# Attention scores' low product over all 128 partitions, and the second selection of two token tiles tied to u tiles

## Chip, cores and metric

The kernel runs on one core of a Trainium2 chip. The metric is the device time of one execution in microseconds (us), as the median of several runs. The engines are named as in the profile: PE is TensorE's matmuls, PEld its weight loads, DVE is VectorE, ACT is ScalarE, POOL is GpSimd, SP issues DMAs. Each engine executes its own instructions in order and waits on semaphores of the others.

## What is computed

One layer of an encoder over 512 tokens (and 16 meta tokens) of width 1024: differential attention with 4 heads of twice 64 channels, a bidirectional gated linear attention beside it, an output projection, and then a feed-forward part that picks 16 of 16384 single-neuron experts for each token and head through product keys. Cut to what the change touches:

```python
s = jnp.einsum('bqhcd,bkhcd->bhcqk', qi, k).astype(jnp.float32)       # scores of the two halves c, d = 64
p = jax.nn.softmax(s, axis=-1)
a = p[:, :, 0] - lam * p[:, :, 1]
...
def peer_ffn(x, w_q, sub_keys, u, v):
    q = (xi @ w_q).reshape(n, PEER_HEADS, 2, PEER_KEY_DIM)
    s = jnp.einsum('nhpc,hpkc->nhpk', q, sub_keys).astype(jnp.float32)
    ts, ti = lax.top_k(s, PEER_TOPK)                                  # first selection: 16 of 128, twice
    cand_s = (ts[:, :, 0, :, None] + ts[:, :, 1, None, :]).reshape(n, PEER_HEADS, PEER_TOPK * PEER_TOPK)
    best_s, best_p = lax.top_k(cand_s, PEER_TOPK)                     # second selection: 16 of the sums
    idx = jnp.take_along_axis(cand_i, best_p, axis=-1)
    gate = jax.nn.softmax(best_s, axis=-1)
    act = jax.nn.gelu(jnp.einsum('nd,nhkd->nhk', xi, u[idx]).astype(jnp.float32), approximate=False)
    return jnp.einsum('nhk,nhkd->nd', (gate * act).astype(xi.dtype), v[idx])
```

## The kernel before

Precise products are made of three fast ones: a value is split into a rounded high part and the rest, the low part (ACT copies, then DVE or POOL subtracts: L118 and L120 for streamed weights), and high by high, high by low and low by high are added up in PSUM (`mm3`, L131 to L133).

The program has these stages. The front (to about 355 us) normalises, projects, and runs the attention (`attn_unit`, one for each of 4 heads and 4 tiles of 128 tokens) and the linear attention between the streamed projections, then the output projection. From there to about 470 us come the query projection of the feed-forward part and the first selection (`top16`: MAX8, FIND_INDEX8, MATCH_REPLACE8, MAX8, FIND_INDEX8 for each row). The u phase (470 to 765 us) multiplies three of the four token tiles with all experts: 60 u tiles of 24 matmuls in its first part (`u_tile`), whose streamed weights are split by DVE or, for the first `LP` of them, by POOL (`u_split`). The v phase (795 to 1606 us) multiplies the activations with the other expert matrix. Token tile 0 goes another way: its experts are gathered row by row by POOL's indirect DMAs, and DVE works on the rows.

For token tiles 1 to 3 the gates of the selected experts are spread into a dense matrix by matmuls with one-hot tiles. That is done by 48 building steps (`wbuild`) woven into the u tiles: step n of 8 tokens stands behind u tile `tgt(n)` = `A0` + int(0.56 n), and `AG` later from step n = `AL` = 14 on. A step needs one comparison and one product on DVE (`oh`, L1024 and L1029, four buffers), 16 matmuls on PE (L1060, L1063) and copies on ACT. The first step of a token tile transposes that tile's selection on PE (L1002: gate, row and column, from `sel`). Steps are prepared one ahead, so the transposes of tile 2 are asked for at the step with n = 15.

The second selection (`topk2`, L194) runs on DVE for two token tiles a and one half of the heads b at a time: a conversion (`tf`), three additions that make 80 candidates for each head, `top16` for each of 8 heads, some ten small row operations, then twice a comparison with 16 positions (L239), a product (L243), three halving additions (L245) and a write to `sel` (L247). Last the gate is made (`fin`, L250: an exponential on ACT, a sum, a reciprocal and a product, L255). Tiles 0 and 1 are one such pair (a = 0), of which the second half, (0, 1), is done ahead of the building steps; tiles 2 and 3 (`late`, L964 and L1043) are the pairs (1, 0) and (1, 1), written in the program between steps 13 and 14.

What sets the order: Tile's scheduler orders each engine's instructions by a simulated timeline and by the dependencies of data. Added dependencies of kind ORDER_DEP (`anchors[i]` is the last matmul of u tile i, `gelus[i]` its activation) only fix an order in that list.

In `attn_unit` each half c of a head has two matmuls into one bank: the low part of the keys over the 64 rows of that half (L490), then the high part over 128 rows (L491), where the query tile `stq` holds the high part in 64 rows and the low part in the other 64.

## Time and profile before

| | us |
|---|---|
| median of 3 runs (lowest, highest) | 1622.23 (1618.59, 1625.28) |
| the profiled execution | 1627.63 |
| its span | 1625.9 |
| PE busy | 1559.1 (96%) |
| DVE busy | 1265.5 (78%) |
| ACT busy | 714.2 (44%) |
| POOL busy | 538.0 (33%) |

The mean granted clock of TensorE is 0.981 of full speed. A share of busy time is a mean over stages with different limits, so the rows below are read by stretch. In a timeline the columns are start, duration, engine, line, operation, output and inputs, shapes; matmuls overlap in the pipeline, so what one costs is read from start to start. In square brackets stands how long the engine was idle ahead of a row, and what it waited for.

### The profile page before, as it was taken

Reading aid. Unit: us, or ns where it says so; the run is one execution under the profiler, and the core shown is the slowest. Engines: PE = TensorE matmul, PEld = TensorE weight load, DVE = VectorE, ACT = ScalarE, POOL = GpSimd, SP = SyncE. Lnnn points to the kernel's source line nnn. Section 1 sums busy time; section 2 is a strip of 40 time slices with the busy share of each in tenths; the row PEclk is TensorE's granted clock in tenths of the full one; section 3 lists DMA queues with packets and bytes.
Section 4 is the critical chain, followed back from the end, with each engine's and each line's share of the span. In section 5 each row is a group of like instructions: output and inputs, shape, how many; then the busy total and the mean of one; then the engine's idle time right before and its main releaser. Section 6 shows DMA issues by size and latency. Waiting matters only on the chain.

```text
span 1625.9 us, 24038 instructions
## 1 busy us (share of the span) xinstructions
PE 1559.1 (96%) x8793; PEld 1382.0 (85%) x8793; DVE 1265.5 (78%) x2492; ACT 714.2 (44%) x1131; POOL 538.0 (33%) x419
## 2 busy tenths in 40 slices
PE   6999999999996799998999999999999999999997
PEld 6887886778896799998888888889999999999996
DVE  3888767657999986993477777798878888788896
ACT  5444654544332476884333333333333333333333
POOL 3445113048553001000012222255445554344442
PEclk9999998999998899999999999999999999999998
DMA  6112122233233376879999988899999999999975
GB/s 234 61 48 84 59 61 70 81 108 106 92 128 112 115 264 228 309 285 341 338 312 304 328 321 286 290 388 343 351 346 333 331 339 346 351 324 339 335 256 181
DMA packets 152358, 387.40 MB, mean 238 GB/s; under 512 B 12752, under 2 KB 71376, under 8 KB 150576
## 3 DMA queue, kind: packets, MB, share of 16 engines
q1 hardware_dynamic: 104432, 213.62, 38.3%
q0 software_dynamic: 36864, 134.23, 22.9%
q10 hardware_dynamic: 10944, 38.02, 6.2%
q8 instruction: 69, 1.13, 0.3%
q14 instruction: 49, 0.40, 0.1%
HBM read 342.56 MB, written 40.63 MB: 236 GB/s over the span
## 4 chain that ended last, share of the span: by engine, by line
PE 73%; DVE 14%; DMA 5%; issue 3%; POOL 2%; ACT 2%; SPq 1%; POOLq 0%; ACTq 0%; DVEq 0%
PE bankg L131 10%; PE bankg L132 10%; PE bankg L133 10%; PE banka L1123 7%; PE banka L1122 7%; PE banka L1119 7%; PE bankp L1119 3%; PE bankp L1123 3%; PE bankp L1122 3%; PE banka L1060 1%; PE banka L1063 1%; POOL lo L120 1%; PE banka L656 1%; PE banka L491 1%; PE banka L490 1%
## 5 line engine op out<-in xcount | busy, mean ns | idle before, releaser
L264 POOL DMA_INDIRECT gat<-u,idx x128 | 166.3, 1300 | 568.8 <-PE bankp L1123 243.1
L118 ACT CAST hi<-raw 128x1024 fp32r<-128x1024 f32 x177 | 186.1, 1053 | 308.9 <-PE bankg L132 224.2
L131 PE MATMUL bankg<-un_hi,hi 128*128 128x384 f32 x896 | 302.9, 338 | 5.4 <-ACT act L1094 5.4
L133 PE MATMUL bankg<-un_hi,lo 128*128 128x384 f32 x896 | 302.3, 338 | 0.0
L132 PE MATMUL bankg<-un_lo,hi 128*128 128x384 f32 x896 | 302.0, 337 | 0.0
L120 DVE TENSOR_TENSOR lo<-raw,hi 128x1024 fp32r<-128x1024 f32 x142 | 174.0, 1227 | 97.8 <-ACT hi L118 96.1
L264 POOL DMA_INDIRECT gat<-v,idx x128 | 169.2, 1322 | 182.2 <-PE bankp L1123 155.0
L139 DVE TENSOR_TENSOR vhl<-vraw,vhl 128x1024 fp32r<-128x1024 f32 x128 | 156.3, 1221 | 51.6 <-ACT vhl L138 51.5
L278 DVE CUSTOM_DVE_ANT_0 gat<-gat,hn 128x1024 f32<-128x1024 f32 x128 | 155.2, 1221 | 42.3 <-DMA gat<-u,idx 42.2
L131 PEld LDWEIGHTS bankg<-un_hi,hi 128*128 128x128 f32 x896 | 169.4, 189 | 9.4 <-ACT act L1094 5.7
L138 ACT CAST vhl<-vraw 128x1024 fp32r<-128x1024 f32 x128 | 134.2, 1049 | 93.1 <-PE bankp L1123 53.2
L132 PEld LDWEIGHTS bankg<-un_lo,hi 128*128 128x128 f32 x896 | 169.3, 189 | 3.2
L133 PEld LDWEIGHTS bankg<-un_hi,lo 128*128 128x128 f32 x896 | 169.3, 189 | 1.7
L276 DVE SCALAR_TENSOR_TENSOR acc<-gat,sact,acc 128x1024 f32<-128x1024 f32 x128 | 163.9, 1280 | 5.0 <-DMA gat<-v,idx 4.0
L120 POOL TENSOR_TENSOR lo<-raw,hi 128x1024 fp32r<-128x1024 f32 x35 | 85.4, 2442 | 68.7 <-ACT hi L118 68.6
L1065 ACT ACTIVATE stg<-banka 128x512 f32<-128x512 f32 x96 | 96.3, 1171 | 11.7 <-PE banka L1063 10.5
L1094 ACT ACTIVATE act<-bankg 128x384 f32<-128x384 f32 x112 | 54.5, 486 | 32.3 <-PE bankg L133 27.2
L1024 DVE TENSOR_TENSOR oh<-iT,ioh 128x2048 f16<-128x2048 f16 x48 | 56.9, 1216 | 0.4 <-PE banka L1063 0.4
L1029 DVE TENSOR_TENSOR oh<-oh,gs 128x2048 f16<-128x2048 f16 x48 | 56.9, 1216 | 0.0
L1060 PE MATMUL banka<-oh 128*128 128x128 f16 x384 | 48.6, 220 | 0.9 <-ACT stg L1065 0.5
L131 PE MATMUL bankg<-act_hi,hi 128*128 128x264 f32 (+1 forms) x144 | 47.3, 328 | 1.3 <-ACT vN L777 1.3
L1063 PE MATMUL banka<-oh 128*128 128x128 f16 x384 | 48.2, 219 | 0.0
(2287 smaller groups left out, 3771.7 us busy)
## 6 DMA issues: line engine op xcount, KB each, us to landing
raw<-uT SPq DMA_DIRECT2D x128, 512.0 KB
vraw<-v SPq DMA_DIRECT2D x128, 512.0 KB
W_d<-stg ACTq DMA_DIRECT2D x12, 2048.0 KB
wa<-W_d SPq DMA_DIRECT2D x32, 768.0 KB
A_d<-act ACTq DMA_DIRECT2D x60, 192.0 KB
wa<-A_d SPq DMA_DIRECT2D x15, 768.0 KB
raw<-wq SPq DMA_DIRECT2D x16, 512.0 KB
raw<-win_n SPq DMA_DIRECT2D x12, 512.0 KB
```

Of the source, the lines that this page charges most:

```text
L118: nc.scalar.copy(hi, raw)
L120: (eng or nc.vector).tensor_sub(lo, raw, hi.bitcast(F32))
L131: nc.tensor.matmul(o, lhsT=ah, rhs=bh, start=start, stop=False)
L132: nc.tensor.matmul(o, lhsT=ah, rhs=bl, start=False, stop=False)
L133: return nc.tensor.matmul(o, lhsT=al, rhs=bh, start=False, stop=stop)
L139: (eng or nc.vector).tensor_sub(lo, src, hi.bitcast(F32))
L264: g = nc.gpsimd.indirect_dma_start(out=r, out_offset=None, in_=src, in_offset=bass.IndirectOffsetOnAxis(ap=idx[:, hk:hk + 1], axis=0))
L276: nc.vector.scalar_tensor_tensor(acc0, r, sact[:, hk:hk + 1], acc0, op0=ALU.mult, op1=ALU.add)
L278: nc.vector.tensor_tensor_reduce(r, r, hn0, scale=1.0, scalar=0.0, op0=ALU.mult, op1=ALU.add, accum_out=sact[:, hk:hk + 1])
L1119: m0 = nc.tensor.matmul(o, lhsT=gh_[:, tc_], rhs=vh[:, dc], start=(j == 0), stop=False, skip_group_check=True)
L1122: nc.tensor.matmul(o, lhsT=gh_[:, tc_], rhs=vl[:, dc], start=False, stop=False, skip_group_check=True)
L1123: m = nc.tensor.matmul(o, lhsT=gl_[:, tc_], rhs=vh[:, dc], start=False, stop=(j == NK - 1), skip_group_check=True)
```

## The change

1. The low part of the keys is written to `klz`, four tiles of 128 rows (one for each half, for two heads in turn), in which the other half's 64 rows are zeroed once at the beginning by POOL copies of zeros. The low product takes all 128 rows of the query tile. To make room, the pool tag `q` has 3 buffers instead of 4, `glan` lies inside `acc0`, and some small tiles (`mx`, `nb`, `zt`, `rz`, `sf`, `em`, `kmn`, not shown in the diff) have one buffer less.
2. The late second selections are tied: the conversion and the three additions of (1, 0) are ordered behind u tile 17 and those of (1, 1) behind u tile 22.
3. POOL subtracts for u tiles 0 to 11 and 18 to 28, instead of 0 to 13.
4. `A0` is 10 instead of 11 and `AG` 11 instead of 10: the building steps of tile 1 begin one u tile earlier, those behind `AL` stay.

```diff
@@ -51,7 +51,7 @@
 RB = 2
-TBUF = {'e': 3, 'g': 6, 'q': 4, 'x': 2}
+TBUF = {'e': 3, 'g': 6, 'q': 3, 'x': 2}
 GA = 4
@@ -77,10 +77,11 @@
 PG = 33, 49, 1
-LP = 14
-A0 = 11
+LP = 12
+LQ = 18, 29
+A0 = 10
 AR = 0.56
-AG = 10
+AG = 11
 AL = 14
@@ -191,15 +192,18 @@
-    def topk2(a, b, sm, cand, tf, eq, zs):
+    def topk2(a, b, sm, cand, tf, eq, zs, behind=None):
         ts_ = tsv[:, b, 2 * a:2 * a + 2].rearrange("p t h c r -> p (t h) c r")
         ti_ = tiv[:, b, 2 * a:2 * a + 2].rearrange("p t h c r -> p (t h) c r")
-        nc.vector.tensor_copy(tf, ti_[:, :, :, :, None].to_broadcast([P, PH, 2, TOPK, 2]))
-        nc.vector.tensor_add(cand[:, :, 0:16], ts_[:, :, 1, :], ts_[:, :, 0, 0:1].to_broadcast([P, PH, 16]))
-        nc.vector.tensor_add(cand[:, :, 16:72].rearrange("p h (a b) -> p h a b", b=8),
-                             ts_[:, :, 1, None, 0:8].to_broadcast([P, PH, 7, 8]),
-                             ts_[:, :, 0, 1:8, None].to_broadcast([P, PH, 7, 8]))
-        nc.vector.tensor_add(cand[:, :, 72:80], ts_[:, :, 0, 8:16], ts_[:, :, 1, 0:1].to_broadcast([P, PH, 8]))
+        ops = [nc.vector.tensor_copy(tf, ti_[:, :, :, :, None].to_broadcast([P, PH, 2, TOPK, 2])),
+               nc.vector.tensor_add(cand[:, :, 0:16], ts_[:, :, 1, :], ts_[:, :, 0, 0:1].to_broadcast([P, PH, 16])),
+               nc.vector.tensor_add(cand[:, :, 16:72].rearrange("p h (a b) -> p h a b", b=8),
+                                    ts_[:, :, 1, None, 0:8].to_broadcast([P, PH, 7, 8]),
+                                    ts_[:, :, 0, 1:8, None].to_broadcast([P, PH, 7, 8])),
+               nc.vector.tensor_add(cand[:, :, 72:80], ts_[:, :, 0, 8:16], ts_[:, :, 1, 0:1].to_broadcast([P, PH, 8]))]
+        if behind is not None:
+            for o_ in ops:
+                tc.add_manual_dep(o_.ins, anchors[behind], ORDER_DEP, reason="order")
         bsv = sm("bsv")
@@ -392,6 +396,11 @@
+    klz = [[f1.tile([P, T], F32R, name=f"klz{j}{c}") for c in range(2)] for j in range(2)]
+    for kz in klz:
+        for c in range(2):
+            nc.gpsimd.tensor_copy(kz[c][64 - 64 * c:128 - 64 * c], rrs[0][64 - 64 * c:128 - 64 * c, :T])
+
     def proj_rope(c, meta):
@@ -406,12 +415,12 @@
         st_ = [f2.tile([P, T], F32R, name=f"st{'qk'[meta]}{j}") for j in range(2)]
-        lo = f2.tile([P, T], F32R, name="stl") if meta else tz("sql", [P, T], F32R)
+        lo = klz[c % 2] if meta else [tz("sql", [P, T], F32R)] * 2
         for j in range(2):
...
             nc.scalar.copy(st_[j][r], dst[r, :T])
-            nc.gpsimd.tensor_sub(lo[r], dst[r, :T], st_[j][r].bitcast(F32))
-            nc.sync.dma_start(out=st_[j][x].bitcast(F32), in_=(st_[j] if meta else lo)[r].bitcast(F32))
+            nc.gpsimd.tensor_sub(lo[j][r], dst[r, :T], st_[j][r].bitcast(F32))
+            nc.sync.dma_start(out=st_[j][x].bitcast(F32), in_=(st_[j] if meta else lo[j])[r].bitcast(F32))
         return dst, st_, lo
@@ -448,7 +457,7 @@
     nc.vector.tensor_scalar(subw, subw, 1.0 - LAM0, None, op0=ALU.mult)
-    glan = f1.tile([P, P], F32, name="glan")
+    glan = acc0[:, D - P:]
     nc.sync.dma_start(out=glan, in_=I["glan"].to_broadcast([P, P]))
@@ -486,13 +495,12 @@
         for c in range(2):
-            rows = slice(64 * c, 64 * c + 64)
-            nc.tensor.matmul(s[c], lhsT=qs_[c][rows, qc], rhs=kl[rows, :], start=True, stop=False)
+            nc.tensor.matmul(s[c], lhsT=qs_[c][:, qc], rhs=kl[c], start=True, stop=False)
             nc.tensor.matmul(s[c], lhsT=qs_[c][:, qc], rhs=ks[c], start=False, stop=True)
@@ -925,12 +933,12 @@
-    def topk2w(a, b):
+    def topk2w(a, b, behind=None):
         def sm(name, dt=F32):
...
         return topk2(a, b, sm, tk2.tile([P, PH, NCAND], F32, name="cand"), tk2.tile([P, PH, 2, TOPK, 2], BF, name="tf"),
-                     tk1.tile([P, PH * 8, 2 * TOPK], BF, name="eq", tag="gat", bufs=GA), tk2.tile([P, PH], F32, name="zs"))
+                     tk1.tile([P, PH * 8, 2 * TOPK], BF, name="eq", tag="gat", bufs=GA), tk2.tile([P, PH], F32, name="zs"), behind)
@@ -1040,8 +1048,9 @@
             if n == AL:
-                for ab in late:
-                    for _ in topk2w(*ab):
+                for j, ab in enumerate(late):
+                    yield tgt(n) - AG + j * AG // 2
+                    for _ in topk2w(*ab, behind=tgt(n) - AG + j * AG // 2):
                         pass
@@ -1070,7 +1079,7 @@
         if i < NK and i not in U:
-            U[i] = stream(I["uT"][i], eng=nc.gpsimd if i < LP else None)
+            U[i] = stream(I["uT"][i], eng=nc.gpsimd if i < LP or LQ[0] <= i < LQ[1] else None)
```

Three places in the engines' orders, of which steps of the prediction speak. The first is DVE, up to the last write of the gates of tile 1 (the second `sel` write with `sm_gate`, which the transposes of tile 1 wait for). In the kernel before, `cand_5973` and `sm_..5949` to `5982` belong to the late selections, `cand_4790`, `eq_4792` and `zs_4243` to the tiles 0 and 1; the stretch runs through the middle of it:

```order
L239 TENSOR_TENSOR eq_4792<-sm_cb_4858,io16b_76 128x2048
L232 TENSOR_TENSOR sm_cf_5948<-sm_cf_5948,sm_bsv_5955 128x128
L234 TENSOR_SCALAR sm_rf_5947<-sm_rf_5947 128x128
L243 TENSOR_TENSOR eq_4792<-eq_4792,tf_4791 128x2048
L233 TENSOR_TENSOR sm_cb_5950<-sm_cf_5948,sm_t9_5953 128x128
L188 MAX sm_bsv_5981<-cand_5973 128x8
L235 TENSOR_TENSOR sm_rb_5949<-sm_rf_5947,sm_t9_5953 128x128
L188 MAX sm_bsv_5981<-cand_5973 128x8 x7
L245 TENSOR_TENSOR eq_4792<-eq_4792 128x64x16
L197 CAST tf_5974<-tiv_3808 128x512
L189 MAX_INDEX sm_bp_5982<-sm_bsv_5981,cand_5973 128x8
L239 TENSOR_TENSOR eq_5893<-sm_rb_5949,io16b_76 128x2048
```

In the changed kernel, from the same comparison of `cb` to the writes of `sel` (its L259 is L255 of before, L243 is L239, L249 is L245, L121 is L120):

```order
L243 TENSOR_TENSOR eq_4795<-sm_cb_4861,io16b_76 128x2048
L247 TENSOR_TENSOR eq_4795<-eq_4795,tf_4794 128x2048
L249 TENSOR_TENSOR eq_4795<-eq_4795 128x64x16
L249 TENSOR_TENSOR eq_4795<-eq_4795 128x64x8
L249 TENSOR_TENSOR eq_4795<-eq_4795 128x64x4
L251 TENSOR_TENSOR sel_3793<-eq_4795 128x2x64
L1000 SCALAR_TENSOR_TENSOR idx_3794<-sel_3793 128x128
L257 TENSOR_REDUCE zs_4246<-sm_gate_4413 128x8
L258 RECIPROCAL zs_4246<-zs_4246 128x8
L259 TENSOR_TENSOR sel_3793<-sm_gate_4413,zs_4246 128x2x64
L259 TENSOR_TENSOR sel_3793<-sm_gate_4852,zs_4796 128x2x64
L121 TENSOR_TENSOR lo_5277<-raw_5273,hi_5275 128x1024
```

Nothing of the late selections stands ahead of the writes any more. In the whole order, 16 each of the five operations of `top16` have moved behind them, two sets of conversion and additions, one set of ten row operations, and one each of L239, L243 and the three of L245. All of it now stands behind the comparison and product of step 13.

The second place is PE, around the transposes of tile 1 (L1002 before, L1010 in the changed kernel). Before, they stand inside u tile 12, after row 2328 of PE's order:

```order
L131 MATMUL bankg_5371<-un_hi_3809,hi_5272 128x384
L132 MATMUL bankg_5371<-un_lo_3810,hi_5272 128x384
L1002 MATMUL bankp_5310<-ident_67,sel_3790 128x128 x3
L133 MATMUL bankg_5371<-un_hi_3809,lo_5274 128x384
L131 MATMUL bankg_5452<-un_hi_3809,hi_5306 128x384
```

In the changed kernel they stand between u tiles 10 and 11, after row 2283:

```order
L133 MATMUL bankg_5245<-un_lo_3813,hi_5199 128x384
L134 MATMUL bankg_5245<-un_hi_3812,lo_5201 128x384
L1010 MATMUL bankp_5279<-ident_67,sel_3793 128x128 x3
L132 MATMUL bankp_5340<-un_hi_3812,hi_5241 128x384
L133 MATMUL bankp_5340<-un_lo_3813,hi_5241 128x384
```

They are 44 matmuls (1.83 u tiles) earlier. The building steps of tile 1 move with them, from u tile 16.6 to 30 before to u tile 14.1 to 30; the transposes of tile 2 stand at u tile 30.0 in both.

The third place is POOL, at the end of its subtractions (L120 before, L121 in the changed kernel; L264 and L268 are the gathers). Before:

```order
L940 TENSOR_TENSOR hk<-hk,hrow 128x384 x2
L120 TENSOR_TENSOR lo<-raw,hi 128x1024
L139 TENSOR_TENSOR un_lo<-hk,un_hi 128x384 x2
L120 TENSOR_TENSOR lo<-raw,hi 128x1024 x19
L264 DMA gat<-u,idx 128x1024 x128
```

In the changed kernel:

```order
L121 TENSOR_TENSOR lo<-raw,hi 128x1024
L140 TENSOR_TENSOR un_lo<-hk,un_hi 128x384 x2
L121 TENSOR_TENSOR lo<-raw,hi 128x1024 x27
L268 DMA gat<-u,idx 128x1024
L121 TENSOR_TENSOR lo<-raw,hi 128x1024
L268 DMA gat<-u,idx 128x1024 x127
```

Nine more subtractions (23 of u tiles, 14 before) stand there, the last behind the first gather.

## Rows read from the trace of the kernel before

**Rows 1.** Busy time by stretches: engines with busy us and instructions, clock, DMA.
```profile
core 0: us, PE busy (x) PEld busy (x) DVE busy (x) ACT busy (x) POOL busy (x), PEclk, DMA share, GB/s
160.00:200.00 40.00, 40.00 (x300) 34.16 (x298) 28.67 (x66) 26.06 (x71) 8.90 (x10) 1.00 0.19 58
520.00:560.00 40.00, 21.43 (x136) 21.04 (x137) 40.00 (x133) 8.66 (x13) 0.00 (x0) 0.72 0.18 60
800.00:1200.00 400.00, 399.13 (x1879) 344.88 (x1878) 309.24 (x453) 143.85 (x198) 131.57 (x106) 1.00 0.91 323
```
**Rows 2.** Waits of PE, 460 to 790 us: total, times, longest.
```profile
PE bankp L1002 <- DVE sel L255: 24.5, 1, 24.5
PE bankg L131 <- ACT act L1094: 5.4, 1, 5.4
```
**Rows 3.** Timeline of PE around the transposes of tiles 1 and 2.
```profile
511.68 0.33 PE L132 MATMUL bankg<-un_lo,hi 128*128 128x384 f32 x1
...
513.24 0.33 PE L132 MATMUL bankg<-un_lo,hi 128*128 128x384 f32 x1
...
538.57 0.90 PE L1002 MATMUL bankp<-ident,sel 128*128 128x128 f32 x3 [24.47 <-DVE sel L255]
...
539.58 0.52 PE L131 MATMUL bankg<-un_hi,hi 128*128 128x384 f32 x1
...
627.94 0.49 PE L1002 MATMUL bankp<-ident,sel 128*128 128x128 f32 x3
```
**Rows 4.** Timeline of PE at one score pair, between other matmuls of 512 columns.
```profile
312.59 0.39 PE L132 MATMUL bankg<-mix_lo,hi 128*128 128x512 f32 x1
312.82 0.39 PE L133 MATMUL bankg<-mix_hi,lo 128*128 128x512 f32 x1
313.13 0.49 PE L490 MATMUL banka<-stl,stq 64*128 64x512 f32 x1
313.56 0.50 PE L491 MATMUL banka<-stk,stq 128*128 128x512 f32 x1
313.89 0.39 PE L131 MATMUL bankg<-mix_hi,hi 128*128 128x512 f32 x1
```
**Rows 5.** Line L490: duration in ns (min/median/max), first and last start.
```profile
L490 PE MATMUL banka<-stl,stq x32: 468/497/792, 155.8 to 316.1; 64*128 64x512 f32 x32
```
**Rows 6.** Timeline of POOL, the first 45 us.
```profile
21.38 0.20 POOL L350 CAST am<-act_hi 128x16 fp32r<-128x16 f32 x1 [7.09 <-ACT act_hi L342]
```
**Rows 7.** Chain of waits, 490 to 640 us: start, us on the chain, what.
```profile
495.49 1.15 DVE sm_bsv L188 x8
...
497.90 1.69 DVE sm_bp L189 x8
...
523.42 1.13 DVE eq L243
```
**Rows 8.** Timeline of DVE in the middle of a second selection.
```profile
519.66 0.67 DVE L245 TENSOR_TENSOR eq<-eq 128x1024 bf16<-128x1024 bf16 x1
520.25 0.21 DVE L220 TENSOR_SCALAR sm_row<-sm_bp 128x128 uint32<-128x128 uint32 x1
```
**Rows 9.** Timeline of POOL, 405 to 640 us.
```profile
466.25 2.39 POOL L120 TENSOR_TENSOR lo<-raw,hi 128x1024 fp32r<-128x1024 f32 x1 [4.44 <-ACT hi L118]
...
508.59 2.40 POOL L120 TENSOR_TENSOR lo<-raw,hi 128x1024 fp32r<-128x1024 f32 x1 [2.83 <-ACT hi L118]
...
606.59 1.14 POOL L264 DMA_INDIRECT gat<-u,idx  x1 [95.61 <-PE bankg L133]
```
**Rows 10.** Timeline of DVE beside subtractions of POOL.
```profile
416.24 2.38 DVE L199 TENSOR_TENSOR cand<-tsv 128x448 f32<-128x448 f32 x1
...
467.12 2.60 DVE L243 TENSOR_TENSOR eq<-eq,tf 128x2048 bf16<-128x2048 bf16 x1
...
509.36 1.78 DVE L232 TENSOR_TENSOR sm_cf<-sm_cf,sm_bsv 128x128 f32<-128x128 f32 x1
```
**Rows 11.** Timeline of POOL in the front, two groups of three operations.
```profile
114.71 1.98 POOL L674 TENSOR_TENSOR ef<-pre 128x256 f32<-128x256 f32 x3 [2.23 <-DVE pre L641]
119.48 8.48 POOL L675 TENSOR_TENSOR ef<-pre 128x256 f32<-128x256 f32 x3 [2.79 <-DVE pre L641]
```

More of the change, by code (lines that the diff above doesn't have):

```diff
@@ L503, in attn_unit @@
                                  accum_out=z[:, 2 + c:3 + c])
-        zt = f2.tile([P, 2], F32, name="zt", bufs=4)
+        zt = f2.tile([P, 2], F32, name="zt", bufs=3)
         nc.vector.scalar_tensor_tensor(zt, z[:, 2:4], 0.5, z[:, 0:2], op0=ALU.mult, op1=ALU.add)
-        rz = f2.tile([P, 2], F32, name="rz", bufs=4)
+        rz = f2.tile([P, 2], F32, name="rz", bufs=3)
         nc.vector.reciprocal(rz, zt)
-        sf = f2.tile([P, 1], F32, name="sf", bufs=4)
+        sf = f2.tile([P, 1], F32, name="sf", bufs=3)
         nc.vector.scalar_tensor_tensor(sf, zt[:, 0:1], nlam, rz[:, 1:2], op0=ALU.mult, op1=ALU.mult)
@@ L714, in gla_pair @@
             if dr == 0:
-                em = f2.tile([P, 2, NM], F32, name="em")
+                em = f2.tile([P, 2, NM], F32, name="em", bufs=1)
                 mb = [P, 2, NM]
@@ L721, in gla_pair @@
                 nc.tensor.transpose(out=bm2[:2 * NM, :P], in_=em.rearrange("p j m -> p (j m)"), identity=ident)
-                kmn = f2.tile([2 * NM, P], F32, name="kmn")
+                kmn = f2.tile([2 * NM, P], F32, name="kmn", bufs=1)
                 nc.scalar.copy(kmn, bm2[:2 * NM, :P])
```

4 lines of the change are left out of this document (2 added, 2 removed).

## The prediction

> **What bounds the kernel now.** I read the busy time by stretches first, to see where TensorE does not run; then its waits in the weak stretch; then the rows at both ends of that wait; then the chain of waits, for who is late there. In the stretches [rows 1] TensorE is full from 160 to 200 us and in the v phase (399.13 of 400 us). The hole is 520 to 560: 21.43 of 40 us, clock 0.72, while VectorE is busy for the whole 40 and GpSimd for none. From 460 to 790 us TensorE has two waits worth naming [rows 2]: 24.5 us, once, for `sel`, and 5.4 us at the change to the v phase, which the edit does not touch. The first is the transposes of the tile 1 selection [rows 3]: they start at 538.57, and the matmuls behind them last 0.52 us instead of 0.33 (the lower of the two clock levels, 1.2 GHz, after the idle time) for a few us, about 1.3 us more in all. So three things set the end: TensorE's amount of work wherever it is full, VectorE up to 538.5 us, and again TensorE from there on.
>
> **The change part by part.** *Low product over 128 partitions.* Per score pair, the starts are 0.31 us (into the low product), 0.43 (to the high one) and 0.33 (to the next) apart, against 0.23 between neighbours that use all 128 rows [rows 4]: 1.07 against 0.69, so 0.38 us of excess. There are 32 pairs [rows 5], hence 12 us. With all 128 rows the pair looks like its neighbours, and the same number of columns goes through. They lie between 155.8 and 316.1 us [rows 5], where TensorE is full in part, and waits in part near 270 and 290. I take three quarters, X = 9 us; the bounds are 13 (all of it, with the pairs at the lower clock) and 0 (the cost is not of the 64 rows, or another engine ends last). Making the zeros and the smaller pools I cost at nothing: the four GpSimd copies stand in the first microseconds, where GpSimd waits for data before its `am` copies, and again for 7.09 us at 21.38 [rows 6]; without that cover they would cost up to 1.2 us each, half of what GpSimd takes for twice the columns [rows 9]. One `q` buffer fewer can hold back one evacuation in the projections by an estimated 1 us; the 3 us that I leave out of X cover it.
>
> *The tie.* VectorE executes in order, and ahead of the last write of tile 1's `sel` it now does one and a bit of the late selections. The order of the changed kernel takes from there two top-16 sets (16 heads), two preparations, one set of row operations, and one comparison, one product and one reduction. From the rows: 8 heads cost 1.15 + 1.69 + 1.69 + 1.15 + 1.69 = 7.37 us [rows 7] (MAX8 twice, the other three operations like FIND_INDEX8), so 14.7 for 16; the comparison and the product 1.13 each [rows 7]; the three halving additions 0.59 from start to start and then about half each time [rows 8], 1.1; ten row operations of up to 0.2 each [rows 8], 1.6; two preparations, estimated at 1.2 each from that length and the columns of the four operations, 2.4. Together 22. GpSimd's subtractions for u tiles 12 and 13 go to VectorE behind this point, and with them about 3 us in which VectorE stood behind GpSimd (below). So `sel` would be ready at 538.5 − 25 = 513.5 − X.
>
> *A0 one smaller.* TensorE's transposes come 44 matmuls earlier in its order; at 0.173 us (nine in 1.56 us [rows 3]) that is 7.6 us. Before, it arrived at 538.57 − 24.5 = 514.1; now at 506.5 − X. It therefore still waits, 7 us in place of 24.5, and what it gains is 17. The same by position: the kernel of before would be where TensorE resumes at 538.5 − 7.6 = 531 us, and now is at 513.5 − X.
>
> *Tile 2 next.* TensorE needs the selection of tile 2 at u tile 30, 19 tiles after the first transposes: 19 × 24 × 0.173 = 79 us, plus 15 building steps at about 1.1 us, plus 1.8 for transposes and clock: s + 97, with s the time when the first `sel` is ready. (The same sum for before gives 538.6 + 89.5 = 628; the row says 627.94 [rows 3], without a wait.) VectorE has now all of both late selections behind s: the building steps are paced by TensorE until about s + 45; then come 35 us of selection (two sets, each of a top-16 at 7.4, preparation 1.2, row operations 2, and twice 3.6 for comparison, product, reductions and write; a small part earlier), and three subtractions and one reduction; the exponentials of the gate are held behind u tile 27 anyway. That makes s + 88, or s + 93.5 by the hold. There is cover of 9 us.
>
> *LQ.* 11 subtractions for u tiles 18 to 28 move to GpSimd, at 2.39 to 2.41 us each [rows 9] against 1.14 on VectorE; nine in all leave VectorE net. GpSimd idles there (95.61 us ahead of the gather at 606.59 [rows 9]). But they are not free for VectorE: beside the GpSimd subtraction at 466.25, the product that takes 1.13 alone takes 2.60 [rows 10], ending with it; at 508.59 the small addition takes 1.78 [rows 10]. Of the 19 subtractions between 404 us and the last at 508.59 [rows 9], 13 held a VectorE operation (the first at 416.24, the last at 509.36 [rows 10]), by 1.65 us on average: c = 1.1 us for each. MAX8 and its kin were not held. The second stall is then max(0, 11c − 9): 3 us at c = 1.1; 9 at 1.65; 17 at 2.4, where each is held for a whole subtraction. I take c = 1.1, since half of the selection's time is MAX8 and its kin, as in those rows.
>
> The rule in the Trainium skill, "SBUF — State Buffer", section Who interferes with whom, speaks against this part: a VectorE operation with two inputs in SBUF and a GpSimd operation that reads it take turns, each for its whole instruction. The held product agrees [rows 10]; by the rule taken for each of the 11, the second stall would be the 17 us.
>
> *The sum.* Gain 17 + 9 − 3 = 23, less 1 for the smaller items: 22 us. 1627.6 − 22 = 1605.6 against the profiled run; that run lies 5.4 us above the median, so 1600 in terms of medians. From 640 us to the end all moves rigidly: TensorE is full in the v phase [rows 1].
>
> **The rivals.** (A) *The held subtractions take back the cover.* VectorE is nearly full from s on; with c = 2.4 the second stall is 17 and the gain 9: 1613. For it: the 1.13 us product held to 2.60. Against: 6 of 19 held nothing. (B) *No front gain.* If the extra time at the pairs comes of the weights' loading or another engine ends last there, X is 0 to 2, and 17 + 1 − 3 − 1 = 14 gives 1608. For it: TensorE is not full near 270. Against: neighbours with the same load lie 0.23 apart [rows 4]. (C) *GpSimd is starved.* Back-to-back VectorE operations with two inputs kept three GpSimd operations for 8.48 us that took 1.98 elsewhere [rows 11]; `lo` of u tiles 18 to 20 comes late and TensorE waits, up to 10 us, until the building steps' four buffers stop VectorE: about 1610. (D) *Slower: both engines stretch each other.* If a subtraction takes its 2.4 us from VectorE and another 2 us are lost in taking turns (from 8.48 / 3 less the 0.7 of the others [rows 11]), c is 4.4, the stall at tile 2 is 11 × 4.4 − 9 = 39 us, and 26 − 39 = −13: 1635. It decides from c = 3.9, (26 + 8 + 9) / 11. Against: no row of VectorE beside a GpSimd subtraction was held for longer than that one's own time. (E) *The tie does nothing* for tile 1: then only the front remains, and 7.6 us earlier arrival only lengthens the wait: 1613. Against: the order shows the top-16 sets behind the write of `sel`.
>
> **How the numbers follow.** A measurement of this kernel can tell about 0.5%, 8 us, from no change. Chances: forecast (1591 to 1605) 0.50; A 0.14; B 0.11; C 0.10; E 0.02; A with B, which ends at 1622, 0.09; D 0.04. The cases above 1614 are A with B, D, and a part of A, C and E: same 0.13, slower 0.04, faster 0.83. The predicted time is the forecast's. The range runs from 1590 (front 13, no second stall) to 1616 (A with 3 us on top), and leaves out A with B, D, and little of the rest.
>
> **What would show it.** After: the low and the high product 0.23 us apart, and the stretch to 320 us shorter by about X; the wait for `sel` 5 to 10 us, once, with a shorter time at the low clock; VectorE's L188 rows of the late sets behind the first building steps; GpSimd subtractions spread over 540 to 600 us, VectorE rows of 1.5 to 2.6 us beside them; the second transposes with a wait of 0 to 5 us. A long second wait speaks for A or D; waits of TensorE on `lo` for C; unchanged pair spacing for B. I am wrong if the first wait does not shrink, or if the v phase itself becomes longer.

## The result and the profile after

The changed kernel takes 1613.85 us (median of 5, 1610.16 to 1615.14) against 1625.28 for the kernel before on the same chip (median of 5): a ratio of 0.9923, 95% interval 0.9901 to 0.9945, so 9 to 16 us faster. The forecast was 22 us. The profiled executions are 1627.63 and 1614.99 us, 12.6 apart. The median lies in the range; the size of the gain is little more than half of what was forecast, and the parts of the sum fell out differently from that.

The score pairs first. The timeline of PE shows one pair of the changed kernel among the same neighbours as [rows 4] (L498 and L499 are L490 and L491 of before, L132 to L134 are L131 to L133):

```profile
303.38 0.40 PE L134 MATMUL bankg<-mix_hi,lo 128*128 128x512 f32 x1
303.61 0.39 PE L498 MATMUL banka<-klz,stq 128*128 128x512 f32 x1
303.84 0.39 PE L499 MATMUL banka<-stk,stq 128*128 128x512 f32 x1
304.07 0.39 PE L132 MATMUL bankg<-mix_hi,hi 128*128 128x512 f32 x1
```

All starts are 0.23 us apart; the excess of 0.38 us for a pair is gone. What that does to the front is seen on GpSimd: its subtraction that stood at 415.74 us stands at 402.96 (first row before, second after, from the timelines of POOL):

```profile
415.74 2.40 POOL L120 TENSOR_TENSOR lo<-raw,hi 128x1024 fp32r<-128x1024 f32 x1 [1.24 <-ACT hi L118]
```
```profile
402.96 2.40 POOL L121 TENSOR_TENSOR lo<-raw,hi 128x1024 fp32r<-128x1024 f32 x1 [1.18 <-ACT hi L119]
```

X is 12.8 us between these two executions, but not all of it is the pairs. The front of the kernel before also ran longer at the lower of TensorE's two clock levels (columns as in [rows 1], first before, then after):

```profile
240.00:280.00 40.00, 36.31 (x190) 26.99 (x189) 31.15 (x76) 19.98 (x43) 14.66 (x11) 0.95 0.30 83
280.00:320.00 40.00, 39.71 (x173) 28.38 (x172) 27.42 (x76) 22.09 (x69) 0.00 (x0) 0.88 0.17 54
```
```profile
240.00:280.00 40.00, 35.67 (x180) 27.23 (x180) 32.59 (x78) 20.76 (x51) 14.60 (x11) 0.91 0.26 71
280.00:320.00 40.00, 38.45 (x210) 31.22 (x209) 30.94 (x98) 23.99 (x72) 0.00 (x0) 1.00 0.28 86
```

By an estimate, 40 us at a granted clock of 0.88 are worth 35.2 at full speed. From 120 to 320 us (120 to 160 stands at 0.96 before and 1.00 after) that makes 8.4 us lost before and 3.6 after, so some 5 us of X are the clock. The first pair starts 1.4 us later than before (157.2 against 155.8 us), and about 9 us are left for the pairs. A run below, in which the excess of the pairs stays and the clock does not fall, agrees. Whether the shorter spell at the lower clock follows from the change is not shown: from 150 to 330 us the same estimate gives 0 to 3.5 us in the eleven profiled kernels with the new product, 8.5 and 10.2 in two with the old one, and 0 in that run.

The waits of PE from 450 to 790 us (total, times, longest) answer to [rows 2]; L1010, L259 and L121 are L1002, L255 and L120 of before:

```profile
PE bankp L134 <- DVE lo L121: 9.0, 1, 9.0
PE bankp L1010 <- DVE sel L259: 7.6, 1, 7.6
PE bankg L132 <- ACT act L1103: 5.6, 1, 5.6
PE banka L1069 <- DVE oh L1037: 3.6, 2, 2.6
```

The wait for the selection of tile 1 is 7.6 us instead of 24.5, and it ends at 501.3 us. A wait of 9.0 us is new, and it is for the low part of a u tile, not for a selection. By stretches (columns as in [rows 1]) the hole of 520 to 560 us has closed, and a smaller one has opened from 560 to 640:

```profile
520.00:560.00 40.00, 38.95 (x348) 37.34 (x347) 38.22 (x49) 33.31 (x38) 13.21 (x5) 1.00 0.68 257
560.00:600.00 40.00, 35.19 (x214) 34.71 (x212) 39.52 (x156) 13.40 (x19) 18.14 (x8) 0.97 0.45 154
600.00:640.00 40.00, 33.20 (x241) 32.27 (x242) 31.08 (x40) 23.82 (x29) 8.36 (x1) 0.86 0.64 229
800.00:1200.00 400.00, 399.89 (x1886) 345.83 (x1885) 311.61 (x459) 144.42 (x198) 135.69 (x110) 1.00 0.92 328
```

To follow the gain, set TensorE's time at one place of its order against that of before. At u tile 11.0, after the first wait, it is 531.0 - 501.3 = 29.7 us ahead (12.8 of the front, 16.9 of the selection; forecast 26). The 531.0 is 538.6 less the 7.6 us of 44 matmuls: the kernel before passed that place ahead of its wait, and is counted as if the wait lay behind it. At the transposes of tile 2 it is 627.94 [rows 3] - 609.83 = 18.1 us ahead, at those of tile 3 14.3, at the first matmul of the v phase 13.5, and at the end 12.7. So 11.6 us go between u tiles 11 and 30, where 3 were forecast (9.0 of wait, 1.0 of a short wait for `oh` at 543 us, the rest at the lower clock), and 3.8 between 30 and 39, where none were. The timeline of PE shows the ends of the two waits and the transposes between them:

```profile
604.20 0.69 PE L134 MATMUL bankp<-un_hi,lo 128*128 128x384 f32 x1 [9.01 <-DVE lo L121]
604.68 0.52 PE L132 MATMUL bankp<-un_hi,hi 128*128 128x384 f32 x1
...
609.83 0.49 PE L1010 MATMUL bankp<-ident,sel 128*128 128x128 f32 x3
...
635.50 0.29 PE L1069 MATMUL banka<-oh 128*128 128x128 f16 x1 [2.61 <-DVE oh L1037]
```

After each wait TensorE runs at the lower of its two levels for a few us (0.52 us for a matmul of 0.33), which adds over 1 us each time.

What VectorE does meanwhile, beside GpSimd's subtractions (first the timeline of POOL, then that of DVE):

```profile
554.28 3.40 POOL L121 TENSOR_TENSOR lo<-raw,hi 128x1024 fp32r<-128x1024 f32 x1 [3.08 <-ACT hi L119]
...
565.90 2.42 POOL L121 TENSOR_TENSOR lo<-raw,hi 128x1024 fp32r<-128x1024 f32 x1 [1.01 <-ACT hi L119]
```
```profile
532.75 4.56 DVE L1037 TENSOR_TENSOR oh<-oh,gs 128x2048 f16<-128x2048 f16 x2
...
546.26 2.34 DVE L1037 TENSOR_TENSOR oh<-oh,gs 128x2048 f16<-128x2048 f16 x2
...
565.98 2.48 DVE L233 SCALAR_TENSOR_TENSOR sm_t<-sm_rf,sm_cf 128x128 f32<-128x128 f32 x1
...
602.93 1.22 DVE L121 TENSOR_TENSOR lo<-raw,hi 128x1024 fp32r<-128x1024 f32 x1
...
607.28 0.49 DVE L259 TENSOR_TENSOR sel<-sm_gate,zs 128x128 f32<-128x128 f32 x2
```

The operation at 565.98 takes 0.28 us elsewhere; here it lasts as long as the subtraction that began 0.08 us ahead of it. Two products take 4.56 us where two others take 2.34. Nine such places stand between 532 and 586 us, and what they take above their time without a neighbour adds up to 17 us, 1.9 for each place: c = 1.55 us for each of the 11 subtractions. The last write of the late selections ends at 607.8, that is s + 106.5 with s = 501.3; by the formula of the prediction, 88 + 11 x 1.55 = 105. And the subtraction for u tile 29, which VectorE kept, stands at 602.93 within the selections, so TensorE stops one tile ahead of the transposes.

The 2.6 us at 635.50 have their cause on another queue (timeline of POOL, then of DVE):

```profile
619.88 8.36 POOL L268 DMA_INDIRECT gat<-u,idx  x1 [34.93 <-PE bankg L134]
```
```profile
626.21 1.22 DVE L1032 TENSOR_TENSOR oh<-iT,ioh 128x2048 f16<-128x2048 f16 x1
631.93 1.22 DVE L282 CUSTOM_DVE_ANT_0 gat<-gat,hn 128x1024 f32<-128x1024 f32 x1 [4.51 <-DMA gat<-u,idx]
```

VectorE's work on a gathered row stands in its order ahead of a building pair, and waits 4.5 us for the row; TensorE waits for the pair. In the kernel before, the gather at the same place took GpSimd 4.78 us and VectorE waited 3.2 us for it, but TensorE did not wait.

That the row comes late has its cause on VectorE. It runs two-input operations without a gap from 619.4 to 627.4 us, and the issue on GpSimd ends 0.8 us behind that, at 628.2. It is the same 0.8 us in the kernel before (642.0 and 642.8) and in three runs below. By these rows VectorE itself holds up the gather on which it then waits.

### The profile page after: what moved, and what is told of

Read it like the earlier page. It is cut to its first block, busy times and chain, and to the rows that moved or that the text cites. A ratio compares the mean times of both kernels' runs of the same rounds, so it can differ in the third digit from the quotient of the medians.

```text
span 1613.2 us, 24039 instructions
## 1 busy us (share of the span) xinstructions
PE 1550.2 (96%) x8793; PEld 1385.2 (86%) x8793; DVE 1269.6 (79%) x2483; ACT 713.9 (44%) x1131; POOL 563.1 (35%) x432
## 3 DMA queue, kind: packets, MB, share of 16 engines
q8 instruction: 69, 1.13, 0.3%
## 4 chain that ended last, share of the span: by engine, by line
PE 58%; issue 3%; DMA 3%; DVE 3%; ACT 1%; POOL 1%; SPq 0%; ACTq 0%; POOLq 0%; DVEq 0%
PE bankg L132 8%; PE bankg L133 7%; PE bankg L134 7%; PE banka L1132 7%; PE banka L1128 7%; PE banka L1131 7%; PE bankp L1128 3%; PE bankp L1131 3%; PE bankp L1132 3%; DMA gat<-u,idx 1%; PE banka L1069 1%; PE banka L1072 1%; DMA gat<-v,idx 1%; PE bankp L132 1%; PE bankp L133 1%
## 5 line engine op out<-in xcount | busy, mean ns | idle before, releaser
L268 POOL DMA_INDIRECT gat<-u,idx x128 | 169.1, 1321 | 479.1 <-PE bankp L1132 236.1
L132 PE MATMUL bankg<-un_hi,hi 128*128 128x384 f32 x896 | 303.2, 338 | 5.6 <-ACT act L1103 5.6
L133 PE MATMUL bankg<-un_lo,hi 128*128 128x384 f32 x896 | 301.8, 337 | 0.0
L134 PE MATMUL bankg<-un_hi,lo 128*128 128x384 f32 x896 | 301.8, 337 | 0.0
L121 DVE TENSOR_TENSOR lo<-raw,hi 128x1024 fp32r<-128x1024 f32 x133 | 164.0, 1235 | 92.0 <-ACT hi L119 90.2
L268 POOL DMA_INDIRECT gat<-v,idx x128 | 169.4, 1323 | 182.6 <-PE bankp L1132 155.3
L132 PEld LDWEIGHTS bankg<-un_hi,hi 128*128 128x128 f32 x896 | 169.4, 189 | 9.6 <-ACT act L1103 5.9
L133 PEld LDWEIGHTS bankg<-un_lo,hi 128*128 128x128 f32 x896 | 169.4, 189 | 3.2
L134 PEld LDWEIGHTS bankg<-un_hi,lo 128*128 128x128 f32 x896 | 169.1, 189 | 1.6
L121 POOL TENSOR_TENSOR lo<-raw,hi 128x1024 fp32r<-128x1024 f32 x44 | 110.6, 2513 | 129.3 <-ACT hi L119 129.2
L1103 ACT ACTIVATE act<-bankg 128x384 f32<-128x384 f32 x112 | 54.3, 485 | 30.8 <-PE bankg L134 25.8
L1037 DVE TENSOR_TENSOR oh<-oh,gs 128x2048 f16<-128x2048 f16 x48 | 62.1, 1330 | 0.0
L134 PE MATMUL bankp<-un_hi,lo 128*128 128x384 f32 x128 | 44.4, 347 | 9.0 <-DVE lo L121 9.0
L1069 PE MATMUL banka<-oh 128*128 128x128 f16 x384 | 48.9, 221 | 3.8 <-DVE oh L1037 3.6
L132 PE MATMUL bankg<-act_hi,hi 128*128 128x264 f32 (+1 forms) x144 | 47.6, 331 | 1.3 <-ACT vN L785 1.3
```

Of the source, the lines that this page charges most:

```text
L121: (eng or nc.vector).tensor_sub(lo, raw, hi.bitcast(F32))
L132: nc.tensor.matmul(o, lhsT=ah, rhs=bh, start=start, stop=False)
L133: nc.tensor.matmul(o, lhsT=ah, rhs=bl, start=False, stop=False)
L134: return nc.tensor.matmul(o, lhsT=al, rhs=bh, start=False, stop=stop)
L268: g = nc.gpsimd.indirect_dma_start(out=r, out_offset=None, in_=src, in_offset=bass.IndirectOffsetOnAxis(ap=idx[:, hk:hk + 1], axis=0))
```

## The experiments

The line numbers are those of each run's own kernel, where an edit can shift them by a few (the transposes, L1010 in the changed kernel, are L1006 and L1011 in two of the runs). Ratios are to the kernel before on the same chip, with 95% intervals.

**The low product alone** (the constants and `late` as before):

```diff
-LP = 12
-LQ = 18, 29
-A0 = 10
+LP = 14
+LQ = 0, 0
+A0 = 11
-AG = 11
+AG = 10
...
-                for j, ab in enumerate(late):
-                    yield tgt(n) - AG + j * AG // 2
-                    for _ in topk2w(*ab, behind=tgt(n) - AG + j * AG // 2):
+                for ab in late:
+                    for _ in topk2w(*ab):
```

> The low product over 128 partitions alone, with the smaller pools; selection, splits and building steps as in the kernel before. Theory (the front's gain is passed on whole): in the changed kernel GpSimd's subtraction that stood at 415.74 us stands at 402.96, so 12.8 us; the wait for the selection of tile 1 stays 24.5 us, and the whole is 12 to 13 us faster, ratio 0.992. Rival (my forecast's size): 9 us, with part of the pairs off the path. Rival (later stages take it back, as they did with the selection's gain): under 5 us.

Measured: 1612.87 us, ratio 0.9929 (0.9902 to 0.9956), 7 to 16 us faster. The wait of PE is the old one:

```profile
PE bankp L1010 <- DVE sel L259: 24.5, 1, 24.5
```

So the front's gain is passed on whole, and it alone is as large as that of the full change.

**The other three parts alone** (the tiles and the pools of the front also as in the kernel before, not shown):

```diff
-            nc.tensor.matmul(s[c], lhsT=qs_[c][:, qc], rhs=kl[c], start=True, stop=False)
+            rows = slice(64 * c, 64 * c + 64)
+            nc.tensor.matmul(s[c], lhsT=qs_[c][rows, qc], rhs=kl[rows, :], start=True, stop=False)
```

> The other three parts alone (tie, subtractions of u tiles 18 to 28 on GpSimd, building steps one u tile earlier); low product over 64 partitions as before. Theory (all that the tie gains is lost behind it: first wait 7.6 instead of 24.5, then about 9 us for a low part of u tile 29, 2.6 behind a gather, and the lower clock after both): within 3 us of the kernel before. Rival (the later losses exist only because the front is shorter): 10 to 14 us faster.

Measured: 1624.3 us, ratio 1.0004 (0.9985 to 1.0022). The waits of PE (450 to 790 us):

```profile
PE bankp L134 <- DVE lo L121: 10.1, 1, 10.1
PE bankp L1006 <- DVE sel L259: 7.6, 1, 7.6
```

The first wait is 17 us shorter here too, and all of it is lost behind it, without any help of the front. The two runs add up to the whole change.

**GpSimd's subtractions left out.** This run tells most: the 11 subtractions go, and the orders of VectorE and TensorE stay up to the last write of the selections, but for one gathered row, which VectorE works on some operations earlier.

```diff
-            U[i] = stream(I["uT"][i], eng=nc.gpsimd if i < LP or LQ[0] <= i < LQ[1] else None)
+            if LQ[0] <= i < LQ[1]:
+                raw = fetch(I["uT"][i])
+                hi = stm.tile([P, 1024], F32R, name="hi", tag="hi", bufs=SB)
+                nc.scalar.copy(hi, raw)
+                U[i] = hi, un_lo.rearrange("p k n -> p (k n)")[:, :1024]
+            else:
+                U[i] = stream(I["uT"][i], eng=nc.gpsimd if i < LP else None)
```

> The changed kernel without the 11 subtractions of u tiles 18 to 28: their low part is left out, and TensorE multiplies an old tile in its place. The orders of VectorE and TensorE are those of the changed kernel (transposes of tile 2 at u tile 30.0, the subtraction for u tile 29 behind the late selections), so only what GpSimd's subtractions do to VectorE is taken away. Theory (they hold VectorE for 17.5 us in all, c = 1.6, and the stall at tile 2 is 11c less a cover of 9 us): the last write of the late selections 15 to 18 us earlier, no wait for the low part of u tile 29 (0 to 1 us instead of 9.0), 10 to 14 us faster than the changed kernel, 1600 to 1604. Rival (VectorE's order and its own work are the bound): a wait of 5 us or more stays, and the time is 1608 or more.

Measured: 1595.02 us, ratio 0.9818 (0.9789 to 0.9846), 19 us below the median of the changed kernel (17 by the ratios) and below the 1600 to 1604 that were expected. Waits of PE from 450 to 830 us, and the last write on DVE:

```profile
PE bankp L1010 <- DVE sel L259: 7.6, 1, 7.6
PE bankg L132 <- ACT act L1109: 5.2, 1, 5.2
```
```profile
590.81 0.49 DVE L259 TENSOR_TENSOR sel<-sm_gate,zs 128x128 f32<-128x128 f32 x2
```

Nothing is left of the waits at tile 2. The first `sel` is ready at 499.7 here, so the last write is at s + 91.6 instead of s + 106.5: 14.9 us, just below the 15 to 18 that were expected. The gain in time is more than the stall of 9.0 us, since the wait behind the gather, the lower clock after two waits and 3 us of waiting in the v phase go with it, and the front happens to be 1.6 us ahead. The rival falls: VectorE's own work and its order leave room.

**The subtractions back on VectorE:**

```diff
-LQ = 18, 29
+LQ = 0, 0
```

> The changed kernel with the subtractions for u tiles 18 to 28 back on VectorE. Theory (each one on GpSimd holds VectorE for 1.6 us, summed from the stretched rows 532 to 586 us): VectorE does 11 x 1.14 = 12.5 us more and is held 17.5 us less, so the second selection is 5 us earlier and the kernel 3 to 5 us faster than the changed one. Rival (what counts is VectorE's own amount of work, the holding is hidden in its waits): 8 to 12 us slower than the changed kernel, about the time before.

Measured: 1603.48 us, ratio 0.9843 (0.9794 to 0.9891), 10 us below the changed kernel's median (13 by the ratios), at least twice what the theory gave. The size is less sure than that: its four executions run from 1589.79 to 1604.81 us. And the theory's number was wrong: the last write of the late selections ends at 607.6, s + 105.1 (s = 502.5 here), nearly as late as in the changed kernel. What differs is the orders. VectorE has the gates ready at 598.4 us, 9 us ahead of the last row or column, where the changed kernel writes the gates last (timeline of DVE):

```profile
597.88 0.49 DVE L259 TENSOR_TENSOR sel<-sm_gate,zs 128x128 f32<-128x128 f32 x2
...
607.35 0.29 DVE L251 TENSOR_TENSOR sel<-eq 128x128 f32<-128x128 bf16 x1
```

And in the order that the scheduler's simulated timeline gives when the subtractions are VectorE's own, the three transposes of tile 2 stand at u tiles 30.8, 31.5 and 32.9, with u tiles between them, so that each waits for its own part alone, and none has to wait (timeline of PE):

```profile
605.67 0.27 PE L1010 MATMUL bankp<-ident,sel 128*128 128x128 f32 x1
...
611.70 0.27 PE L1010 MATMUL bankp<-ident,sel 128*128 128x128 f32 x1
```

**That order taken away again.** The kernel of the last run, with u tiles 30 to 33 behind the transposes:

```diff
+    pin = []
...
+                    if t == 2:
+                        pin.append(m.ins.name)
...
+            for p_ in pin if k == 0 and i < 34 else []:
+                tc.add_manual_dep(m.ins, p_, ORDER_DEP, reason="order")
```

> The kernel e2_nolq (all subtractions from u tile 12 on on VectorE), with TensorE's u tiles 30 to 33 ordered behind the transposes of tile 2, so that these stand at u tile 30.2, as in the changed kernel (30.0), instead of at 30.8 to 32.9. VectorE's order up to the selection stays. Theory (e2_nolq is fast because its transposes stand later in TensorE's order; the selection is ready at the same time, 607.3 us against 607.5, with and without GpSimd): TensorE arrives near 600 us and waits 6 to 9 us, the lower clock costs 1 to 2 more; 7 to 10 us slower than e2_nolq, 1611 to 1614. Rival (e2_nolq is fast because GpSimd no longer holds VectorE): within 2 us of e2_nolq, 1602 to 1606.

Measured: 1613.36 us, ratio 0.9927 (0.9907 to 0.9948), 10 us slower than without the pin. The waits of PE (450 to 790 us) that came back:

```profile
PE banka L1072 <- DVE oh L1040: 7.6, 3, 6.7
...
PE bankp L1011 <- DVE sel L251: 5.1, 2, 4.0
PE banka L1072 <- ACT stg L1077: 1.5, 4, 0.7
PE bankg L134 <- DVE lo L121: 1.3, 1, 1.3
```

VectorE's order up to the selection is that of the last run. So both hold: with GpSimd's share left out nothing stalls at u tile 30, and with VectorE as late as it is, the place in TensorE's order is worth about 10 us. Half of that, 5.1 us, is waiting at the transposes themselves; the rest lies behind them, in short waits for copies and a low part. The wait of 6.7 us for `oh` is not new: the last run had one of 5.7. In both it follows a wait of VectorE for a gather, whose issue on GpSimd took 12.11 us here and 6.00 there. On GpSimd or on VectorE the 11 subtractions make the selection nearly equally late (s + 106.5, s + 105.1, and s + 103.4 here); only with them on VectorE do the engines' orders leave room for it.

**A later place, with GpSimd's subtractions kept** (and none of VectorE's ahead of the selection; AG also moves the tie of (1, 1) from u tile 22 to 23):

```diff
-LQ = 18, 29
+LQ = 18, 33
-AG = 11
+AG = 13
```

> The changed kernel with AG 13 and with GpSimd subtracting for u tiles 18 to 32: the transposes of tile 2 stand two u tiles (8.4 us) later, and no low part is behind the selections on VectorE; GpSimd still holds VectorE. Theory (the position in TensorE's order is what costs): no wait of over 2 us at tile 2, 1601 to 1605. Rival (GpSimd is starved by VectorE's building steps, as in e4_lq_later, where two subtractions took 21.48 us): a wait of TensorE for a low part of 4 to 10 us, 1607 to 1612. Rival (the holding is what costs): the selection is as late as before, and the wait at the transposes stays over 5 us.

Measured: 1611.89 us, ratio 0.9915 (0.9885 to 0.9946). PE waits:

```profile
PE bankp L1010 <- DVE sel L259: 14.5, 2, 7.6
PE banka L1069 <- DVE oh L1037: 9.0, 2, 8.0
```

The theory falls, the last rival holds: 6.9 us of wait are left at the transposes (14.5 less 7.6), since with 15 subtractions the last write ends at 613.4, s + 113. By 88 + 15 x 1.55 it would be 111. But this is only half of the account: the 8.0 us for `oh`, at 717 us, follow a gather whose issue took GpSimd 12.81 us, and without that wait the run would, by an estimate, lie near 1604. That the place helps only if VectorE does not get later with it is therefore argued, not shown.

**Three more subtractions on GpSimd, the place kept:**

```diff
-LQ = 18, 29
+LQ = 18, 32
```

> The changed kernel with GpSimd's subtractions for u tiles 18 to 31 instead of 18 to 28. Theory (TensorE waits 9.0 us for the low part of u tile 29 since VectorE's subtraction for it stands behind the late selections): that wait goes; TensorE then waits at the transposes of tile 2 instead, for the rest of the same selections, less the two subtractions of 1.14 us that VectorE no longer does, 4 to 7 us; 2 to 5 us faster than the changed kernel, 1609 to 1612. Rival (three more subtractions hold VectorE 1.6 us each, so the selection is as late): the same time, with the wait moved to the transposes, 8 to 10 us.

Measured: 1608.33 us, ratio 0.9895 (0.987 to 0.9921), 5 us faster than the changed kernel. The wait for u tile 29 is gone, and 3.8 us at the transposes came in its place, about as expected (4 to 7); another was not (PE's wait, and POOL's timeline):

```profile
PE bankg L134 <- POOL lo L121: 6.2, 1, 6.2
```
```profile
531.46 21.48 POOL L121 TENSOR_TENSOR lo<-raw,hi 128x1024 fp32r<-128x1024 f32 x2 [43.91 <-ACT hi L119]
```

Two subtractions of 2.4 us took 21.48: the first 18.16, the second 3.35. VectorE ran building pairs and then the first additions of a selection without a gap meanwhile, and the first subtraction ended at 549.6, 2.3 us behind the beginning of the first MAX8 rows. That is rival C of the prediction, in a kernel whose orders of the engines differ from the changed one only behind that place. The two waits, 10.0 us, are together no less than the 9.0 that went; the gain fits what else is gone, 3.6 us of waiting for `oh` (the second gather's issue took 2.02 us instead of 8.36), and a front that is 1.3 us ahead.

**The tie undone**, all else as changed:

```diff
-                for j, ab in enumerate(late):
-                    yield tgt(n) - AG + j * AG // 2
-                    for _ in topk2w(*ab, behind=tgt(n) - AG + j * AG // 2):
+                for ab in late:
+                    for _ in topk2w(*ab):
```

> The changed kernel without the tie (late selections free, as before; A0, AG and GpSimd's subtractions as changed). Theory (the tie is what makes the selection of tile 1 early, and it is given back at tile 2): the first wait is 22 to 27 us again, no second one; the time of the low product alone, 1611 to 1615. Rival (A0 alone brings part of it): a first wait of under 20 us and a time below 1608.

Measured: 1625.16 us, ratio 0.9992 (0.9971 to 1.0012). The long wait is back, but at another place, and the time is 10 us above the expected range:

```profile
PE bankg L134 <- DVE lo L121: 22.6, 1, 22.6
...
PE bankg L134 <- POOL lo L121: 3.5, 1, 3.5
```

With the late selections ahead again, TensorE stops until 518.64 us for VectorE's first subtraction, that of u tile 12 (517.35 us, behind the selections), which GpSimd made in the kernel before (`LP` 14 instead of 12). Without the tie the other two edits cost what the low product gains.

**The two low products of a unit side by side**, in the kernel before:

```diff
-            nc.tensor.matmul(s[c], lhsT=qs_[c][rows, qc], rhs=kl[rows, :], start=True, stop=False)
-            nc.tensor.matmul(s[c], lhsT=qs_[c][:, qc], rhs=ks[c], start=False, stop=True)
+            nc.tensor.matmul(s[c], lhsT=qs_[c][rows, qc], rhs=kl[rows, :], start=True, stop=False)
+        for c in range(2):
+            nc.tensor.matmul(s[c], lhsT=qs_[c][:, qc], rhs=ks[c], start=False, stop=True)
```

> The kernel before with the two low products of a unit ahead of the two high ones; in a part of the units the four then follow one another. Theory (the excess of 0.38 us for each pair is the change between 64 and 128 rows): in such a group the second low product follows the first 0.23 us behind, like neighbours of 128 rows, and the excess of the whole group is 0.38 and not 0.76. Rival (each product over 64 rows costs more by itself): 0.4 us between the two low products, 0.76 for the group.

One execution, 1622.04 us. The scheduler puts other work between most of them; at one place the two do follow one another (timeline of PE):

```profile
260.32 0.49 PE L490 MATMUL banka<-stl,stq 64*128 64x512 f32 x2
260.75 0.50 PE L492 MATMUL banka<-stk,stq 128*128 128x512 f32 x1
```

The high product starts 0.43 us behind the first of the two, as it does behind a single one [rows 4]: there the second costs nothing. Both start at 260.3, on different halves of the rows, and run side by side. So this one place fits both the theory and a higher cost of each product over 64 rows, and why the pair costs more stays open; that 128 rows remove the excess is shown.

The run tells something else. Its pairs keep their excess nearly everywhere, yet GpSimd's subtraction that stood at 415.74 us stands at 407.39, 8.4 us earlier than before: TensorE's granted clock is 1.00 from 150 to 330 us. So the front can become 8 us shorter without the pairs. Of these 2.5 us go into a longer wait for the selection (27.0 us).

**Towards a better kernel.** All three keep the low product and the tie, leave the subtractions from u tile 14 on with VectorE, and move the building steps. `A0` moves the tie with them: behind u tiles 19 and 24 with 12, 20 and 25 with 13, instead of 17 and 22. The first:

```diff
-LP = 12
-LQ = 18, 29
-A0 = 10
+LP = 14
+LQ = 0, 0
+A0 = 12
```

> e2_nolq with A0 12 (and GpSimd's first subtractions up to u tile 13 as in the kernel before): the transposes of tile 1 stand at u tile 13, those of tile 2 at 32.8 to 35.2. Theory (the first wait, 7.6 us and 1.3 at the lower clock, is only TensorE's early arrival, and VectorE's work behind it is not the bound): that wait is 0 to 2 us, 6 to 9 us faster than e2_nolq, 1595 to 1598. Rival (VectorE's work from there to the end of the building steps is the bound): the gain comes back as waits for `oh` or for the selections of tiles 2 and 3; within 3 us of e2_nolq.

Measured: 1592.92 us, ratio 0.98 (0.9764 to 0.9837). That is 11 us below the run with the subtractions back on VectorE, more than the theory gave, though the first wait is 3.6 us and not 0 to 2. One of 8.6 is new where the v phase begins, in place of one of 5.8 for `act`:

```profile
PE banka L1128 <- ACT gh__8321 L139: 8.6, 1, 8.6
PE bankp L1010 <- DVE sel L259: 3.6, 1, 3.6
```

The second, against the first:

```diff
-A0 = 12
-AG = 11
+A0 = 13
+AG = 10
```

> e13_a12 with A0 13 and AG 10: the transposes of tile 1 at u tile 14, those of tile 2 at 32.0 to 36.2. Theory (e13_a12 still waits 3.6 us there, and TensorE is the bound behind): that wait goes, 2 to 5 us faster than e13_a12, 1588 to 1591. Rival (the wait of 8.6 us at the beginning of the v phase, which is new in e13_a12, grows by what is gained): within 2 us of e13_a12's 1592.9.

Measured: 1596.45 us, ratio 0.982 (0.9791 to 0.985). Neither holds: at the v phase 4.6 us for `act` are back in place of the 8.6, but 5.6 us for the selection of tile 2 stand in its place:

```profile
PE bankp L1010 <- DVE sel L251: 5.6, 1, 5.6
```

The third, against the first:

```diff
-AG = 11
+AG = 10
```

> e13_a12 with AG 10 instead of 11: the building steps behind the fourteenth one u tile earlier, the transposes of tile 2 at u tile 31.0 to 34.6 (32.8 to 35.2 in e13_a12), the last step one u tile earlier. Theory (e13_a12's remaining 8.6 us at the beginning of the v phase come from the last building steps' late result): that wait falls to 3 to 5 us, 1588 to 1592. Rival (the earlier steps then wait for VectorE, as in e11_pinned): waits of 4 us or more for `oh` or `sel` at tile 2 in its place, 1593 to 1599.

Measured: 1600.57 us, ratio 0.9845 (0.9817 to 0.9874). The theory falls, and the rival with it: the wait at the v phase grows, the one for the building steps is small, and the time is above both ranges:

```profile
PE banka L1128 <- ACT gh__8321 L139: 10.2, 1, 10.2
...
PE banka L1069 <- DVE oh L1037: 2.8, 1, 2.8
```

Where this wait comes from was not settled. The best of the three, A0 = 12 with AG = 11, beats the kernel before by 2.0% and the changed one by 1.2% (0.98 against 0.9923).

## Why the prediction was wrong

- **The front.** X was taken as 9 of 12 us, with a quarter off the path. It is 12.8, and the run of that part alone gives 7 to 16. By the estimate above about 9 of these are the pairs, as forecast, and some 5 are a shorter spell at the lower clock between 270 and 290 us, which the prediction did not have; 1.4 are lost ahead of the first pair; whether by the zeros and the smaller pools, costed at nothing, is not shown. That X comes near the 12 of the full price is luck.
- **The tie and A0.** Right to a microsecond: `sel` was to be ready at 513.5 - X, which is 500.7 with the measured X, and the wait ends at 501.3; the wait was to be 7 us and is 7.6. The gain of the first wait, 17 us, is there in full.
- **Tile 2 and LQ: the step that failed.** The term max(0, 11c - 9) was set to 3 us, with c = 1.1 from rows of 405 to 511 us, where six subtractions in 19 held nothing. In the stretch to which they were moved only two in 11 held nothing, and the others held VectorE for 1.9 us on average instead of 1.65; three of the nine places are building pairs, which the old stretch did not have. So c is 1.55. By the formula itself that is 8 us; measured are 9.0, and about 2 at the lower clock behind them. The left-out subtractions give 14.9 us in place of 11 x 1.55 = 17, and a cover of 6 instead of 9. The cover was too large from the start: the terms listed for VectorE add up to s + 84, the text took s + 88, and beside it stood s + 93.5 by the hold of the exponentials; without the subtractions it was s + 91.6. Rival A put the stall at 17 us with c = 2.4; the truth lies a little less than half way to it.
- **A row misread.** The product held at 467.12 us does not end with the subtraction (468.64) but 1.08 us behind it, at 469.72: it was held and then ran nearly its whole 1.13 us.
- **The place of the stall.** The prediction had TensorE wait at the transposes. It waits one tile ahead, for a subtraction that VectorE kept and that stands in its order within the selections. Who is queued behind the late selections was asked for the transposes, and not for u tiles 29 and 30.
- **"From 640 us on all moves rigidly"** left out 3.8 us between tiles 2 and 3 and over 1 us behind. The second wait also costs a spell at the lower clock, and the building steps of tile 2, with no lead left, then meet a gather that VectorE itself holds up and that used to have slack.
- **The sum.** Forecast 17 + 9 - 3 - 1 = 22. Measured 16.9 + 12.8 = 29.7, less 11.6, 3.8 and 1.6: 12.7. A front that gained 4 more than forecast, by the clock, hides that the losses behind it came to 17 instead of 4.
- **The rivals.** B (no front gain) and E (no tie) did not come about, D (1635) neither: no hold was longer than a subtraction. C is not the cause in the changed kernel, where the slowest subtraction took 3.40 us, but it is real one constant away (18.16 us for one).

Of the change's three other parts together nothing remains; of these, the 11 subtractions on GpSimd cost 17 to 19 us against leaving them out, and 10 to 13 against leaving them with VectorE. The latter is the engines' orders, since VectorE is nearly as late in both.

## What to carry to other kernels

Work that is moved to GpSimd beside a VectorE that runs two-input operations is hardly taken off VectorE: here 11 subtractions made its last write 14.9 us later from GpSimd, and 12 to 13.5 us later on VectorE itself. Measure what a subtraction holds in the stretch to which it goes (1.55 us), not in the one where it happens to be visible (1.1). When a run gains, look at the clock too: some 5 us of this front go with the clock and stood in no term of the sum. When a wait is removed, look for everything queued behind the work that was moved, each engine's small items too, and ask what TensorE needs next of each. A scheduler plans with the durations that it knows; where a delay is not in its plan (a held operation), the place in TensorE's order that it picks can be too early. That this is why the changed kernel's place was too early is a reading of the two orders, which no run tested; that about 10 us hung on the place is measured.

## What the runs showed of the hardware

One subtraction on GpSimd of 2.4 us can take 18.16 us beside two-input operations on VectorE that follow one another without a gap; in the changed kernel the same one, in the same order, took 3.35. Why the one run met it and the other not, the traces do not tell. A gather's issue on GpSimd took 1.14 us at 581 us, and 4.78, 6.00, 8.36, 12.11 and 12.81 beside building pairs of VectorE; in all five it ended 0.8 us behind the end of VectorE's last operation ahead of a gap. And a second matmul over the other 64 rows started with the first: the two took 0.43 us together.
